# Six norm factors in the projection stage of a hybrid encoder layer: spread over the partitions by a round trip through DRAM where matmuls with an identity did it

## Chip, cores, metric

One Trainium2 chip, one core. The metric is the device time of one execution in microseconds, taken over several runs; a lower time is better. A profile was taken of one execution.

## What is computed

One encoder layer over 2048 tokens of width 1024, and a last norm. Cut to what matters here:

```python
h = rmsnorm(x, g_attn)                 # a factor per token: rsqrt(mean(x*x) + 1e-6)
p = h @ w_in                           # 2816 columns
a_b, a_c, a_h = p[0:768]               # mixer A: y_a = a_b * conv3(a_c * a_h)
b_glu = p[768:1280]                    # mixer B:
g = b_glu[:256] * sigmoid(b_glu[256:])
g = causal_dwconv(g, w_conv_b) + b     #   31 taps in depth
y_b = silu(layernorm(g, ln_g, ln_b))   #   mean and a factor per token over 256 channels
q, k, v = p[1280:2816]                 # mixer C: stick-breaking attention, 8 heads of 64
x = x + concat(y_a, y_b, y_c) @ w_out
h2 = rmsnorm(x, g_ffn)
x = x + relu(h2 @ w_ff1)**2 @ w_ff2
return rmsnorm(x, g_final)
```

## The kernel before

Everything is kept transposed: 128 channels on the partitions, 512 tokens along the free dimension, four such blocks of tokens (0 to 3). Each product in full precision is made of three TensorE matmuls in float32r (high by high, low by high, high by low; `mm3`, lines 103, 105 and 107). So each 128x512 output of the projection takes 24 matmuls, and a "group" below is one of these.

**The projection stage** runs in two halves (`p_half(0)`, blocks 0 and 1; `p_half(1)`, blocks 2 and 3). A half goes through eleven weight units: two for mixer B (G), three for mixer A, two each for K, Q and V. Outputs go into PSUM banks with the tag "d", of which there are three, so the TensorE can be at most three groups ahead of the VectorE, which takes each output out of PSUM (`p_evac`, `p_v`). Beside the projection, `weave` advances other generators in step with it: `mixer_b` (the 31 taps on the VectorE, which adds into one PSUM bank with the tag "c", and the layer norm), `x_norms` (sums of squares of x for blocks 2 and 3, in the first half), in the second half the attention of the first token block and `pre_split` (later weights are split into high and low and written to DRAM). A table of numbers in the call of `weave` (cost, start, end) says how fast each is advanced. A scheduler then sets each engine's order of instructions by that program order, by priorities (`tc.high_priority`) and by a simulated timeline; on the chip each engine runs its row strictly in order.

**The attention pieces** need PSUM banks with the tag "z", of which there are two. For each head `a_pass1` asks for three score tiles (`ps_z`, lines 528 and 529) and `a_cross` for one more (`ps_t`, lines 637 to 656, a chain of small VectorE steps). A score tile of the next head has to wait until the VectorE has finished with the bank that it is given.

**The norm factors.** A norm's sum over channels is made by a matmul with ones (`colsum`, line 127), which leaves the sums of 512 tokens as a 128x4 tile: token on the partition. The VectorE scales it (`rs_v`, line 115) and the Pool engine raises it to -1/2 (`rs_y`, line 118). The factor is needed along the free dimension and on all partitions, since the tokens lie there. Before, `spread` does this: four matmuls per norm, each with a column of `rs_y` broadcast as one operand and a 128x128 identity as the other, all in plain float32, into a PSUM tile `ps_R` (line 134). In `norm_spread` the ScalarE copies `ps_R` to an SBUF tile `R` (line 273), which every later evacuation of that token block multiplies by. In `mixer_b` the VectorE multiplies both channel halves (`cb`, line 484) by `ps_R` in PSUM directly; `ps_R` there takes the only "c" bank, in which the next block's taps also add up.

Twelve norms are spread in this way in the program. The six that the change touches are those of `x_norms` (blocks 2 and 3) and of `mixer_b` (blocks 0 to 3). The first two of the projection (`norm_x`), and the four of the later blocks stay as they are.

**Queues.** Loads and stores issued by `self.dma` stand on the queue of the SyncE (SP), which issues in order: where one waits, all behind it wait. `load_r` and the stores of mixer B's output are issued by the Pool engine, in order among its vector instructions.

Of the kernel before, what the change touches and what calls it, by code (L numbers as in the profile page):

```python
# [7 lines left out]
F32 = mybir.dt.float32  # L8
# [7 lines left out]
P = 128  # L16
# [3 lines left out]
TB = 512  # L20
# [9 lines left out]
LN_EPS = 1e-5  # L30
# [38 lines left out]
class Trunk:  # L69
# [78 lines left out]
    def consts(self, ctx):  # L148
        nc, tc, a = self.nc, self.tc, self.a
        c = self.c = ctx.enter_context(tc.tile_pool(name="consts", bufs=1))  # L150
        self.tiny = ctx.enter_context(tc.tile_pool(name="tiny", bufs=2))
        self.dr = ctx.enter_context(tc.tile_pool(name="dr", bufs=1, space=DRAM))
        self.gvec = {}
        t = c.tile([P, DC], F32, name="g_attn")
        nc.scalar.dma_start(t, a["g_attn"].rearrange("(d p) -> p d", p=P))
        self.gvec["g_attn"] = t

        self.ident = c.tile([P, P], F32, name="ident")
        make_identity(nc, self.ident)
        self.ones2 = c.tile([P, 2], F32, name="ones2")  # L160
        nc.vector.memset(self.ones2, 1.0)
        self.mhalf = c.tile([P, 4], F32, name="mhalf")
        nc.vector.memset(self.mhalf, -0.5)
        self.KQ = self.dr.tile([H // 2, 2, P, 3, 2, S // 2], F32, name="KQ")
        self.VS = self.dr.tile([H, S, 2 * HD], F32, name="VS")
        self.Y = self.dr.tile([D, S], F32, name="Y")

        self.WS = self.dr.tile([len(UNITS), 2, P, DC, 256], F32, name="WS")


        self.split_w = {n: self.dr.tile([k, 2, P, 2, DC // 2, P], F32, name="s_" + n) for n, k in (("w_out", DC), ("w1", FC))}
        self.split_w["w2"] = self.dr.tile([FC // G, DC // 2, P, 2, G, 2, P], F32, name="s_w2")
# [71 lines left out]
    def x_norms(self):  # L244

        for g in (2, 3):
            ss = self.mx.tile([P, TB], F32, name="ss", tag="ss", bufs=2)
            for d in range(DC):
                t = self.rp.tile([P, TB], F32, name="xraw", tag=self.rt, bufs=self.rb)
                self.dma(t, self.a["xT"][d * P : (d + 1) * P, g * TB : (g + 1) * TB])  # L250
                self.x_square(ss, t, d, self.nc.gpsimd)
                yield 1
            self.ss[g] = ss
            self.norm_sum(g)
            for _ in range(3):
                yield 1
            self.norm_spread(g)
            yield 1

    def norm_x(self, g):  # L260
        with self.tc.high_priority(offset=HP):
# [185 lines left out]
    def mixer_b(self, hf):  # L447
        nc = self.nc
        for tb in (2 * hf, 2 * hf + 1):
            acc = []  # L450
            for c in range(2):
                while (c, tb) not in self.g:
                    yield None
                g = self.g[c, tb]
                t = self.psum("ps_c", "c")
                nc.vector.tensor_scalar(t, g[:, 0:TB], self.wb[:, c, 0:1], self.vb["b_conv_b"][:, c : c + 1], op0=ALU.mult, op1=ALU.add)
                for k in range(1, 31):
                    nc.vector.scalar_tensor_tensor(t, g[:, k : k + TB], self.wb[:, c, k : k + 1], t, op0=ALU.mult, op1=ALU.add)  # L458
                    if k % 3 == 0:
                        yield 1.8  # L460
                acc.append(self.mx.tile([P, TB], F32, name=f"cb{c}", tag="cb", bufs=2))
                nc.scalar.activation(acc[c], t, AF.Copy)
            for _ in range(3):
                yield 1.8
            mean = self.psum("ps_mean", "c")
            for c in range(2):
                nc.tensor.matmul(mean, self.avg, acc[c], start=c == 0, stop=c == 1)
            sqs = []
            for c in range(2):
                nc.vector.tensor_tensor(acc[c], acc[c], mean, op=ALU.subtract)  # L470
                sq = self.mx.tile([P, TB], F32, name="sq", tag="sq", bufs=2)
                nc.scalar.activation(sq, acc[c], AF.Square)
                sqs.append(sq)
            yield 1.8
            nc.gpsimd.tensor_tensor(sqs[0], sqs[0], sqs[1], op=ALU.add)
            for _ in range(2):
                yield 1.8
            yv = self.rsqrt(self.colsum(sqs[:1], "c"), 1.0 / 256.0, LN_EPS)
            for _ in range(4):
                yield 1.8  # L480
            R = self.spread(yv, "c")
            for c in range(2):
                gg, bb = self.vb["ln_b_g"][:, c : c + 1], self.vb["ln_b_b"][:, c : c + 1]
                nc.vector.tensor_tensor(acc[c], acc[c], R, op=ALU.mult)
                s = self.mx.tile([P, TB], F32, name="sq", tag="sq", bufs=2)
                nc.scalar.activation(s, acc[c], AF.Sigmoid, bias=bb, scale=gg)
                nc.scalar.activation(acc[c], acc[c], AF.Identity, bias=bb, scale=gg)
                nc.gpsimd.tensor_tensor(s, acc[c], s, op=ALU.mult)

                nc.gpsimd.dma_start(self.Y[256 + c * P : 256 + (c + 1) * P, tb * TB : (tb + 1) * TB], s)  # L490
                yield 1.8
# [568 lines left out]
    def build(self):  # L1060
        tc = self.tc
        with ExitStack() as ctx:
            self.consts(ctx)
            self.attention_consts(ctx)
            self.raw = ctx.enter_context(tc.tile_pool(name="raw", bufs=1))
            self.xb = 5
            self.presplit = [("w_out", c, q) for c in range(DC) for q in range(2)] + [("w1", c, q) for c in range(PRE) for q in range(2)]
            self.g, self.u, self.w, self.R, self.rv, self.sig, self.ca, self.ss, self.yraw = ({} for _ in range(9))
            with ExitStack() as c1:
                self.psum_pool(c1, d=3, c=1, z=2, q=1, o=1)  # L1070
                self.p_pools(c1)
                self.w_eng = "dve"
                self.sb = 2
                self.xl = [[None] * DC for _ in range(2)]
                self.xh = [[None] * DC for _ in range(2)]
                with tc.tile_pool(name="raw0", bufs=1) as self.rp:
                    self.rb, self.rt = 21, "raw"
                    self.p_start()
                self.rp = self.raw
                self.rb, self.rt = self.xb, "xt"  # L1080
                self.at = c1.enter_context(tc.tile_pool(name="at1", bufs=1))
                self.ab = dict(Kl=1, A0=6, om=2, Alo=2, Ahi=2, Vl=1, late=1, yc=2)
                weave(self.p_half(0), [(Side(self.mixer_b(0)), 115, 20, 225, True), (Side(self.x_norms()), 24, 60, 180, True)])
                self.heads = {}
                a0 = Side(self.attention([(h, 0) for h in range(H)]))
                weave(self.p_half(1), [(Side(self.mixer_b(1)), 116, 0, 200, True), (a0, 28, 0, 210, True), (Side(self.pre_split(self.presplit[:24])), 24, 0, 200, True), (Side(self.pre_split(self.presplit[24:])), len(self.presplit) - 24, 190, 230, True)])
            with ExitStack() as c2:
                self.psum_pool(c2, d=3, z=3, q=1, o=1)
                self.at = c2.enter_context(tc.tile_pool(name="at2", bufs=1, reuse_waits="tile"))
                self.st = c2.enter_context(tc.tile_pool(name="st2", bufs=1, reuse_waits="tile"))  # L1090
                self.ha = c2.enter_context(tc.tile_pool(name="ha", bufs=1, reuse_waits="tile"))
                self.hp = c2.enter_context(tc.tile_pool(name="hp", bufs=1, reuse_waits="tile"))
                self.ob = 2
                self.kmax = 1536
                self.ab = dict(Kl=1, A0=15, om=2, Alo=3, Ahi=3, Vl=2, late=2, yc=1)
                at = Side(self.attention([(h, i) for i in (1, 2, 3) for h in range(H)]))
                self.heads = {}

                def attend(i):
                    while self.heads.get(i, 0) < H:  # L1100
                        at.advance(at.done + 1)

                self.attend = attend
                self.end = iter(())
                for tb in range(4):
                    weave(self.block(tb, self.end), [(at, (74, 95, 107)[tb], 45, 365 if tb < 2 else 320, False)] if tb < 3 else [])
# [48 lines left out]
```

## Time and profile before

| | us |
|---|---|
| median of three runs | 2396.46 (2393.45 to 2396.71) |
| the profiled execution | 2389.55 |
| its span, first to last instruction | 2387.8 |
| its mean granted TensorE clock | 0.998 |

In the profile, a line of a timeline or of the chain of waits gives the start in us from the span's start, the time in us, the engine, the line of the program, and the operation with output and inputs; "xN" merges N neighbours. In a timeline square brackets give the idle time of that engine just before, and who ended it. A float32 matmul appears as two records, so one `spread` of four matmuls is "x8". Matmuls are pipelined: the recorded time of one runs on while the next has started, so what a matmul costs the TensorE is the distance between starts, not its recorded time. "PEld" is the loading of weights, "SPq" the issue of transfers by the SyncE.

### The profile page before, as it was taken

What the parts mean: (1) busy time and instruction counts of PE and PEld (TensorE: products, weight loads), DVE (VectorE), ACT (ScalarE), POOL (GpSimd) and SP (SyncE); (2) the same over time, 40 slices, a digit from 0 to 9 for tenths busy, and PEclk for the clock granted to TensorE, in tenths of its full rate; (3) what the DMA queues carried; (4) which work ended last, traced back from release to release, by engine and by line L of the source; (5) the groups of instructions that cost most, each with busy time, mean ns of one, the idle gap of its engine ahead of it and who ended that gap; (6) DMA issues with size and microseconds to landing.
All of it is one profiled execution on the core that took longest, in us unless ns stands there. A gap on an engine that the chain in (4) does not pass through costs nothing.

```text
span 2387.8 us, 32873 instructions
## 1 busy us (share of the span) xinstructions
PE 2369.9 (99%) x11316; PEld 2004.1 (84%) x11316; DVE 1500.4 (63%) x2492; ACT 1066.7 (45%) x2002; POOL 1151.7 (48%) x1231
## 2 busy tenths in 40 slices
PE   8999999999999999999999999999999999999998
PEld 7888988898888888888888888888888888888887
DVE  7966698943878777678766668586666525321114
ACT  5232433333566666545555555366555522311221
POOL 1342388731667666427666765278788710000000
PEclk9999999999999999999999999999999999999999
DMA  7569999888778777696677776856676557555545
GB/s 259 205 227 348 294 323 298 285 273 275 191 216 239 204 223 208 210 293 169 210 218 242 232 240 208 277 159 186 192 205 198 168 175 235 175 172 194 198 167 194
DMA packets 238984, 536.49 MB, mean 225 GB/s; under 512 B 27105, under 2 KB 100833, under 8 KB 223457
## 3 DMA queue, kind: packets, MB, share of 16 engines
q1 hardware_dynamic: 180304, 462.01, 57.9%
q0 software_dynamic: 39424, 62.93, 12.0%
q10 hardware_dynamic: 19088, 9.44, 1.4%
q8 instruction: 89, 1.46, 0.2%
q14 instruction: 79, 0.64, 0.1%
HBM read 386.19 MB, written 139.72 MB: 220 GB/s over the span
## 4 chain that ended last, share of the span: by engine, by line
PE 91%; DMA 3%; POOL 2%; issue 2%; DVE 1%; ACT 0%; SPq 0%; POOLq 0%; DVEq 0%; ACTq 0%
PE ps_u L103 10%; PE ps_y L103 10%; PE ps_u L105 10%; PE ps_u L107 10%; PE ps_y L105 10%; PE ps_y L107 10%; PE ps_p L107 4%; PE ps_p L105 3%; PE ps_p L103 3%; PE ps_z L528 3%; PE ps_z L529 3%; PE ps_x L107 2%; PE ps_x L103 2%; PE ps_x L105 2%; PE ps_o L735 2%; PE ps_o L734 2%
## 5 line engine op out<-in xcount | busy, mean ns | idle before, releaser
L90 POOL TENSOR_TENSOR Alo<-A,Ahi 128x512 fp32r<-128x512 f32 x288 | 383.7, 1343 | 90.5 <-ACT Ahi L88 54.3
L984 DVE TENSOR_TENSOR acc<-acc,ps_y 128x512 f32<-128x512 f32 (+1 forms) x264 | 176.0, 668 | 192.6 <-PE ps_y L107 190.2
L103 PE MATMUL ps_y<-fh,w 128*128 128x512 f32 (+1 forms) x1056 | 281.9, 385 | 0.0
L105 PE MATMUL ps_y<-fh,w 128*128 128x512 f32 (+1 forms) x1056 | 280.2, 384 | 0.0
L103 PE MATMUL ps_u<-hh,w 128*128 128x512 f32 x1024 | 278.9, 392 | 1.1 <-ACT hh L903 1.1
L107 PE MATMUL ps_y<-fl,w 128*128 128x512 f32 (+1 forms) x1056 | 279.7, 384 | 0.0
L105 PE MATMUL ps_u<-hh,w 128*128 128x512 f32 x1024 | 277.5, 390 | 0.0
L107 PE MATMUL ps_u<-hl,w 128*128 128x512 f32 x1024 | 277.1, 390 | 0.0
L623 POOL TENSOR_TENSOR A<-A,R 128x512 f32<-128x512 f32 x168 | 223.2, 1331 | 108.1 <-ACT A L621 90.8
L118 POOL TENSOR_TENSOR rs_y<-rs_v,mhalf 128x4 f32<-128x4 f32 (+1 forms) x13 | 13.2, 1017 | 480.5 <-DVE rs_v L117 437.7
L948 ACT ACTIVATE ps_u<-ps_u 128x512 f32<-128x512 f32 x128 | 74.6, 582 | 369.0 <-PE ps_u L107 362.1
L105 PEld LDWEIGHTS ps_y<-fh,w 128*128 128x128 f32 x1056 | 195.1, 188 | 39.6 <-DMA w<-wraw 0.4
L107 PEld LDWEIGHTS ps_y<-fl,w 128*128 128x128 f32 x1056 | 195.1, 188 | 38.8
L105 PEld LDWEIGHTS ps_u<-hh,w 128*128 128x128 f32 x1024 | 192.4, 188 | 40.5
L107 PEld LDWEIGHTS ps_u<-hl,w 128*128 128x128 f32 x1024 | 192.2, 188 | 39.9
L103 PEld LDWEIGHTS ps_y<-fh,w 128*128 128x128 f32 x1056 | 193.2, 188 | 36.5 <-DVE acc L984 0.2
L958 DVE TENSOR_TENSOR fl<-ps_u,fh 128x512 fp32r<-128x512 f32 x128 | 87.8, 686 | 210.6 <-ACT fh L957 210.1
L88 ACT ACTIVATE Ahi<-A 128x512 fp32r<-128x512 f32 x288 | 176.3, 625 | 92.7 <-PE ps_o L734 44.2
L103 PEld LDWEIGHTS ps_u<-hh,w 128*128 128x128 f32 x1024 | 187.5, 188 | 35.9 <-ACT hh L903 1.5
L625 DVE TENSOR_TENSOR R<-ps_z,R 128x512 f32<-128x512 f32 x168 | 115.7, 689 | 134.3 <-ACT ps_z L622 112.5
L458 DVE SCALAR_TENSOR_TENSOR ps_c<-g,wb,ps_c 128x512 f32<-128x512 f32 x240 | 180.1, 750 | 4.9
L90 DVE TENSOR_TENSOR w<-wraw,w 128x512 fp32r<-128x512 f32 x176 | 170.5, 993 | 19.4 <-ACT w L88 17.9
(179 smaller groups left out, 4749.0 us busy)
## 6 DMA issues: line engine op xcount, KB each, us to landing
w<-s_w SPq DMA_DIRECT2D x208, 512.0 KB, 4.0
wraw<-in_w SPq DMA_DIRECT2D x224, 256.0 KB, 4.7
w<-s_w SPq DMA_DIRECT2D x52, 1024.0 KB, 4.8
w<-s_w_out SPq DMA_DIRECT2D x64, 512.0 KB, 4.8
s_w<-w SPq DMA_DIRECT2D x48, 512.0 KB, 5.2
s_w<-w SPq DMA_DIRECT2D x24, 1024.0 KB, 5.9
Qd<-KQ SPq DMA_DIRECT2D x64, 256.0 KB, 6.1
xraw<-in_xT SPq DMA_DIRECT2D x48, 256.0 KB, 4.6
```

The lines of the kernel that those rows point to most:

```text
L88: nc.scalar.activation(hi, x, AF.Copy)
L90: e.tensor_tensor(lo, x, f(hi), op=ALU.subtract)
L103: self.nc.tensor.matmul(ps, wh, xh, start=start and k == 0, stop=False)
L105: self.nc.tensor.matmul(ps, wl, xh, start=False, stop=False)
L107: self.nc.tensor.matmul(ps, wh, xl, start=False, stop=stop and k == n - 1)
L458: nc.vector.scalar_tensor_tensor(t, g[:, k : k + TB], self.wb[:, c, k : k + 1], t, op0=ALU.mult, op1=ALU.add)
L528: nc.tensor.matmul(z[:, oc], keys, g["qh"][:, qc], start=k == 0, stop=False)
L623: nc.gpsimd.tensor_tensor(t, t, R, op=ALU.mult)
L625: nc.vector.tensor_tensor(Rn, z, R, op=ALU.mult)
L948: nc.scalar.activation(ps, ps, AF.Relu)
L958: nc.vector.tensor_tensor(lo, ps, f(hi), op=ALU.subtract)
L984: nc.vector.tensor_tensor(acc[d][:, cols], acc[d][:, cols], ps, op=ALU.add)
```

## The change

A small DRAM tile `NF[k]` (4 by 128) is made for each of the six norms. `put_factors` writes the 128x4 factors to it by a transfer issued by the Pool engine, turned so that the 512 tokens stand in a row; `all_factors` reads this row back by a transfer on the SyncE queue, with the row repeated for all 128 partitions, into an SBUF tile. For `x_norms` that tile is `R` itself, so the copy by the ScalarE goes too. For `mixer_b` it is a new tile `Rc` in the pool's buffers "sq" (two of them, shared with the squares and the sigmoids). The reading transfer has to wait until the writing one has landed. In `mixer_b` the steps between the factor and its use go from four to eight, and the numbers in `weave` follow.

```diff
+        self.NF = [self.dr.tile([4, P], F32, name=f"NF{k}") for k in range(6)]
...
             self.norm_sum(g)
+            self.put_factors(g + 2, self.rv[g])
             for _ in range(3):
                 yield 1
-            self.norm_spread(g)
+            self.R[g] = self.mx.tile([P, TB], F32, name="R", tag="Rs", bufs=4)
+            self.all_factors(self.R[g], g + 2)
             yield 1
+
+    def put_factors(self, k, y):
+        self.nc.gpsimd.dma_start(self.NF[k].rearrange("b p -> p b"), y)
+
+    def all_factors(self, t, k):
+        self.dma(t, self.NF[k].rearrange("b p -> (b p)").unsqueeze(0).to_broadcast([P, TB]))
...
-            yv = self.rsqrt(self.colsum(sqs[:1], "c"), 1.0 / 256.0, LN_EPS)
-            for _ in range(4):
+            self.put_factors(tb, self.rsqrt(self.colsum(sqs[:1], "c"), 1.0 / 256.0, LN_EPS))
+            for _ in range(5):
                 yield 1.8
-            R = self.spread(yv, "c")
+            R = self.mx.tile([P, TB], F32, name="Rc", tag="sq", bufs=2)
+            self.all_factors(R, tb)
+            for _ in range(3):
+                yield 1.8
...
-                weave(self.p_half(0), [(Side(self.mixer_b(0)), 115, 20, 225, True), (Side(self.x_norms()), 24, 60, 180, True)])
+                weave(self.p_half(0), [(Side(self.mixer_b(0)), 123, 20, 225, True), (Side(self.x_norms()), 24, 60, 180, True)])
...
-                weave(self.p_half(1), [(Side(self.mixer_b(1)), 116, 0, 200, True), ...
+                weave(self.p_half(1), [(Side(self.mixer_b(1)), 124, 0, 204, True), ...
```

From the end of the second half on, every engine's order is the same in both programs. Inside the two halves the orders differ, and three places show how. In the rows, names end in numbers that the build gives, and the lines of the changed program lie ten or thirteen higher.

The first place is the TensorE in the first half, where the factors of `mixer_b` for block 0 and of `x_norms` for block 2 are spread between two groups of unit 5 (K). Before:

```order
L107 MATMUL ps_p_1226<-xl1_6_461,wh5_955 128x512
L107 MATMUL ps_p_1226<-xl1_7_475,wh5_955 128x512
L134 MATMUL ps_R_1259<-ident_65,rs_y_1127 128x128 x4
L134 MATMUL ps_R_1277<-ident_65,rs_y_1136 128x128 x4
L103 MATMUL ps_p_1283<-xh1_0_377,wh5_955 128x512
```

The two rows of line 134 are gone in the changed program, and the group behind them follows the one ahead of them at once. In their stead the Pool engine's row now has, just behind the two powers of line 118:

```order
L118 TENSOR_TENSOR rs_y_1101<-rs_v_1102,mhalf_72 128x4
L118 TENSOR_TENSOR rs_y_1143<-rs_v_1144,mhalf_72 128x4
L244 TENSOR_TENSOR ss_1310<-ss_1310,xraw_1378 128x512
L83 DMA Kd_2554<-KQ_74 64x2x256
L265 DMA NF0_77<-rs_y_1101 128x4x1
L83 DMA Kd_2554<-KQ_74 64x2x256
L265 DMA NF4_81<-rs_y_1143 128x4x1
```

Both writes stand among loads of keys (`Kd`); the two reads stand next to one another on the SyncE's queue, between a store of K's high part and one of its low part.

The second place is the VectorE at that same norm. After the change it reads:

```order
L388 TENSOR_TENSOR kq_1261<-ps_p_1236,R_501 128x512
L468 SCALAR_TENSOR_TENSOR ps_c_1373<-g0_1_512,wb_338,ps_c_1373 128x512
L497 TENSOR_TENSOR cb0_712<-cb0_712,Rc_1234 128x512
L497 TENSOR_TENSOR cb1_956<-cb1_956,Rc_1234 128x512
L468 SCALAR_TENSOR_TENSOR ps_c_1373<-g0_1_512,wb_338,ps_c_1373 128x512 x3
L388 TENSOR_TENSOR kq_1296<-ps_p_1271,R_501 128x512
```

The multiplications by the factor now stand between taps of the next block (line 468, adding into `ps_c`): these no longer wait for the bank, and one evacuation (`kq`) stands four rows behind the multiplications. Before, the taps of the next block began only behind them.

The third place is the VectorE in the second half, at block 2's norm, where heads of the attention run beside it. Before, this is the row from the scaled sum (`rs_v`) to the first tap of block 3, with rows left out in the middle:

```order
L115 TENSOR_SCALAR rs_v_3545<-ps_ss_3539 128x4
L371 TENSOR_TENSOR ya_3659<-ps_p_3634,ca_3614 128x512
L709 TENSOR_TENSOR yc_3623<-yc_3623,ps_o_3450 64x512
L637 STREAM_TRANSPOSE ps_t_3560<-R_3372 128x512
...
L656 TENSOR_TENSOR T_3561<-T_3561,ps_t_3560 128x512
...
L484 TENSOR_TENSOR cb0_2921<-cb0_2921,ps_R_3662 128x512
L484 TENSOR_TENSOR cb1_3309<-cb1_3309,ps_R_3662 128x512
...
L456 TENSOR_SCALAR ps_c_3804<-g0_3_2799,wb_332,b_conv_b_334 128x512
```

And after the change:

```order
L669 TENSOR_TENSOR T_3556<-T_3556,ps_t_3555 128x512
...
L115 TENSOR_SCALAR rs_v_3487<-ps_ss_3481 128x4
L381 TENSOR_TENSOR ya_3654<-ps_p_3629,ca_3609 128x512
L466 TENSOR_SCALAR ps_c_3857<-g0_3_2793,wb_338,b_conv_b_340 128x512
...
L652 SCALAR_TENSOR_TENSOR T_3875<-d1_90,ps_t_3874 128x512
L497 TENSOR_TENSOR cb0_2915<-cb0_2915,Rc_3657 128x512
L497 TENSOR_TENSOR cb1_3303<-cb1_3303,Rc_3657 128x512
```

The head whose chain (line 656, now 669) stood behind `rs_v` now stands ahead of it, block 3's taps begin right behind `rs_v`, and the multiplications by the factor stand 28 rows behind it, in the midst of the next head's chain (line 652 is the scan of `a_cross`). On the TensorE the score tiles follow: the three score tiles of the fourth to sixth heads stand 5 to 29 matmuls of the projection earlier in its row than before.

More of the change, by code (lines that the diff above doesn't have):

```diff
@@ L1082, in build @@
                 self.ab = dict(Kl=1, A0=6, om=2, Alo=2, Ahi=2, Vl=1, late=1, yc=2)
-                weave(self.p_half(0), [(Side(self.mixer_b(0)), 115, 20, 225, True), (Side(self.x_norms()), 24, 60, 180, True)])
+                weave(self.p_half(0), [(Side(self.mixer_b(0)), 123, 20, 225, True), (Side(self.x_norms()), 24, 60, 180, True)])
                 self.heads = {}
                 a0 = Side(self.attention([(h, 0) for h in range(H)]))
-                weave(self.p_half(1), [(Side(self.mixer_b(1)), 116, 0, 200, True), (a0, 28, 0, 210, True), (Side(self.pre_split(self.presplit[:24])), 24, 0, 200, True), (Side(self.pre_split(self.presplit[24:])), len(self.presplit) - 24, 190, 230, True)])
+                weave(self.p_half(1), [(Side(self.mixer_b(1)), 124, 0, 204, True), (a0, 28, 0, 210, True), (Side(self.pre_split(self.presplit[:24])), 24, 0, 200, True), (Side(self.pre_split(self.presplit[24:])), len(self.presplit) - 24, 190, 230, True)])
             with ExitStack() as c2:
```

## The prediction

> **What bounds the kernel now.** First the page's table of engines, then the shares of the chain of waits by engine:
>
> ```profile
> PE 2369.9 (99%) x11316; PEld 2004.1 (84%) x11316; DVE 1500.4 (63%) x2492; ACT 1066.7 (45%) x2002; POOL 1151.7 (48%) x1231
> ...
> PE 91%; DMA 3%; POOL 2%; issue 2%; DVE 1%; ACT 0%; SPq 0%; POOLq 0%; DVEq 0%; ACTq 0%
> ```
>
> The TensorE is the bound, with 2369.9 of 2387.8 us. The change lies in the projection, so those stretches come next (busy time of each engine, clock, DMA share):
>
> ```profile
> 300.00:360.00 60.00, 60.00 (x285) 50.20 (x284) 56.05 (x92) 23.41 (x50) 54.00 (x58) 1.00 0.93 317
> 360.00:380.00 20.00, 19.86 (x97) 15.66 (x96) 13.81 (x23) 8.65 (x18) 18.65 (x21) 1.00 1.06 326
> 380.00:400.00 20.00, 19.25 (x97) 16.00 (x96) 19.29 (x32) 9.32 (x18) 16.57 (x19) 1.00 0.96 342
> 400.00:460.00 60.00, 60.00 (x286) 50.18 (x285) 57.49 (x101) 19.60 (x37) 43.80 (x54) 1.00 0.80 254
> ```
>
> The TensorE is full in all of them; the VectorE (third number) is nearly so: 56.05 of 60, 19.29 of 20, 57.49 of 60, with one loose stretch, 13.81 of 20. The granted clock is 1.00 throughout. Then the TensorE's waits from 100 to 560 us; there is one:
>
> ```profile
> PE ps_z L528 <- DVE T L656: 0.7, 1, 0.7
> ```
>
> So a TensorE instruction taken out here is worth its own time, as long as the VectorE does not become the one waited for.
>
> **What is removed.** Six spreads of four float32 matmuls are 24 matmuls, recorded as 48. The group's recorded time, from the groups of 100 to 560 us:
>
> ```profile
> L134 PE MATMUL ps_R<-ident,rs_y 128*128 128x128 f32 x48 | 6.2, 275 | 0.0
> ```
>
> The 6.2 us are not the saving: records of 275 ns overlap. What the TensorE gets back is the distance from the first start of a spread to the start behind it. Its timeline, one pair for each place (the first holds two spreads):
>
> ```profile
> 140.57 1.95 PE L134 MATMUL ps_R<-ident,rs_y 128*128 128x128 f32 x16
> 142.27 0.94 PE L103 MATMUL ps_p<-xh,wh 128*128 128x512 f32 x3
> ...
> 203.19 1.05 PE L134 MATMUL ps_R<-ident,rs_y 128*128 128x128 f32 x8
> 203.99 2.10 PE L103 MATMUL ps_p<-xh,wh 128*128 128x512 f32 x8
> ...
> 252.12 1.05 PE L134 MATMUL ps_R<-ident,rs_y 128*128 128x128 f32 x8
> 252.93 0.36 PE L403 MATMUL ps_v<-wh,xh 128*128 128x256 f32 x1
> ...
> 385.01 1.05 PE L134 MATMUL ps_R<-ident,rs_y 128*128 128x128 f32 x8
> 385.82 1.17 PE L105 MATMUL ps_p<-xh,wl 128*128 128x512 f32 x4
> 386.83 1.55 PE L107 MATMUL ps_p<-xl,wh 128*128 128x512 f32 x6
> 389.12 0.40 PE L528 MATMUL ps_z<-Qd,Kd 128*128 128x256 f32 x1 [0.74 <-DVE T L656]
> ...
> 496.46 1.05 PE L134 MATMUL ps_R<-ident,rs_y 128*128 128x128 f32 x8
> 497.26 0.36 PE L726 MATMUL ps_o<-Ahi,Vd 128*128 128x256 f32 x1
> ```
>
> 1.70 + 0.80 + 0.81 + 0.81 + 0.80 = 4.92 us, some 0.10 us per record. The Trainium skill, "TensorE: Matmul & The Clock Gate", section "Wait — 56ns, not 53.3ns?", gives 55.6 ns from start to start for a warm matmul with 128 columns. By it 48 records would give an estimated 2.7 us, and a time 2.2 us higher than mine; the trace shows about 0.10 us for each, and the measurement decides.
>
> The spread at 385 is a case by itself. 3.3 us behind it the TensorE waits 0.74 us for a VectorE step. If that step comes no earlier, the 0.81 us saved turn into a longer wait. The chain of waits agrees: it runs through the spreads at 140, 252 and 496, but at 385 through the VectorE:
>
> ```profile
> 385.00 1.69 DVE ca L364
> 386.74 1.73 DVE ca L366
> ...
> 390.35 1.15 PE ps_p L103 x5
> ```
>
> So 4.11 us are sure if nothing new waits, and 0 to 0.81 more. I take the middle, 4.5 us, since the change also moves VectorE work at that place, in a direction that may help (below).
>
> The two copies of `ps_R` by the ScalarE go too, and the multiplications read SBUF and not PSUM:
>
> ```profile
> L273 ACT ACTIVATE R<-ps_R x2: 575/586/597, 143.1 to 204.3; 128x512 f32<-128x512 f32 x2
> L484 DVE TENSOR_TENSOR cb<-cb,ps_R x8: 661/680/689, 141.7 to 498.2; 128x512 f32<-128x512 f32 x8
> ```
>
> The copies (2 × 0.59 us) lie beside TensorE work, the ScalarE being busy 23 of 60 us in the rows above: nothing. For the multiplications I take the same 0.68 us. The upper bound is another VectorE multiplication or addition of that size from two SBUF tiles, 0.99 us in the page's groups:
>
> ```profile
> L90 DVE TENSOR_TENSOR w<-wraw,w 128x512 fp32r<-128x512 f32 x176 | 170.5, 993 | 19.4 <-ACT w L88 17.9
> ```
>
> That would be 8 × 0.31 = 2.5 us of VectorE time, 0.6 us at each norm, not on the TensorE's path while evacuations have room. The lower bound is no change.
>
> **What is added.** Twelve DMAs: six writes on the Pool's queue, six reads on the SyncE's. No 2 KB write of single 4-byte elements stands in the trace. The nearest rows are two loads in that form (256 and 1024 single elements), and for the repeated read a load of the same 256 KB into 128 partitions; the last columns are KB and us from issue to landing:
>
> ```profile
> ln_b_g<-in_ln_b_g SPq DMA_DIRECT2D x1, 1.0 KB, 2.1
> g_ffn<-in_g_ffn SPq DMA_DIRECT2D x1, 4.0 KB, 5.0
> xraw<-in_xT SPq DMA_DIRECT2D x48, 256.0 KB, 4.6
> ```
>
> For 512 elements I take 3 us (ends 2.1 and 5.0), for the read 3 us (ends 2.1 and 4.6); six reads of 256 KB beside some 300 GB/s are 5 us of traffic spread over 360 us, so nothing. A handoff thus takes 4 to 10 us where the spread took about 1. The Trainium skill, "DMA: Bandwidth & Descriptors", "Rules for kernel authors", says that a strided last dimension becomes one descriptor per element and that a DMA reading what an earlier one wrote must await its completion; that speaks against this change, and the 2.1 and 5.0 us rows agree that small pieces cost microseconds. It bears on the late-factor rival below.
>
> What waits meanwhile? For `x_norms` (140 and 203) the factor is first used in the second half: hidden. For `mixer_b` blocks 0, 1 and 3 the VectorE has room: at block 0, whose factor was multiplied at 141.7, it waited for the TensorE soon after,
>
> ```profile
> 148.10 0.69 DVE L378 TENSOR_TENSOR kq<-ps_p,R 128x512 f32<-128x512 f32 x1 [0.35 <-PE ps_p L107]
> ```
>
> so that it had no arrears there. A late factor would stop the VectorE, but the TensorE only after up to three banks are full, 3 groups × 24 matmuls × 0.21 us (60.00 us / 285) = 15 us at most. For block 2 the chain is: the power, the write eight Pool instructions behind it, the read on SyncE's queue behind the store of `ya`, the multiplications. In the trace before:
>
> ```profile
> 383.45 1.03 POOL L118 TENSOR_TENSOR rs_y<-rs_v,mhalf 128x4 f32<-128x4 f32 x1
> ...
> 394.00 1.30 POOL L90 TENSOR_TENSOR wpl<-wraw,wph 128x512 fp32r<-128x512 f32 x1 [1.73 <-ACT wph L88]
> ...
> 395.74 0.43 SPq L79 DMA_DIRECT2D Y<-ya  x1
> ...
> 400.25 0.75 DVE L458 SCALAR_TENSOR_TENSOR ps_c<-g,wb,ps_c 128x512 f32<-128x512 f32 x1
> ...
> 409.80 0.68 DVE L378 TENSOR_TENSOR kq<-ps_p,R 128x512 f32<-128x512 f32 x1
> ```
>
> Eight Pool instructions of 0.4 to 1.3 us put the write near 392, its landing near 395, the read behind the store near 396 to 397, and its landing near 400. The multiplications now stand behind some 21 taps of 0.75 us and a dozen other rows, so near 404 to 408. The margin is 4 to 8 us with the middle prices, about 0 to 4 with the upper ones: I take it as hidden. The Pool spends on each write what it spent on another store,
>
> ```profile
> 149.68 0.61 POOL L490 DMA_DIRECT2D Y<-sq  x1
> ```
>
> and it is busy 43.80 of 60 us: hidden.
>
> **What is moved.** Taps of the next block no longer wait for the "c" bank, which fills the loose VectorE stretch at 360 to 380 (6.2 us idle) and makes the crowded one from 400 to 460 lighter. That can end the 0.74 us wait and the smaller gaps around it. On the other hand the score tiles of the fourth to sixth heads stand 5 to 29 matmuls earlier on the TensorE, 1 to 6 us at 0.21 us; unless the VectorE's chain of the head before comes as much earlier, the TensorE waits there. The order has this chain earlier too (line 669 ahead of `rs_v` and not behind). I put these two against each other at zero, with ends of 2 us gained and 4 us lost.
>
> **The sum.** 4.11 + 0.4 = 4.5 us saved. The profiled execution took 2389.55 us, 6.9 us under the median; 2385.05 on its basis, and on that of the median, 2396.46 − 4.5 = 2392.0 us. A difference of about 0.2% (4.8 us) is what a measurement of this kernel can tell from no change, so the forecast lies just inside it.
>
> **The rivals.**
>
> *More is gained.* The earlier taps relieve the VectorE, the wait at 389 and the small gaps around it go. For it speaks the idle 6.2 us at 360 to 380, that taps can fill; against it, that only 0.74 us of waiting are recorded at all. 4.92 + up to 2 = 5 to 7 us: 2389.5 to 2391.5.
>
> *Score tiles eat the gain.* The TensorE now reaches `ps_z` before the VectorE has given the bank back, as it did once at 389. The VectorE's 57.49 of 60 us says that it cannot run ahead by much; against it stands the moved chain. 0 to 4 us saved: 2392.5 to 2396.5.
>
> *The factor comes late at block 2* (the other side). If the Pool's eight instructions include one that waits (it idled 1.73 us for the ScalarE ahead of 394.00 before), or the 4-byte write costs 5 us or more beside weight traffic at DMA share 0.96, then the VectorE stands at the first multiplication, and behind it stand one more `kq` evacuation, taps and the scan's followers of a head. The TensorE loses time once the evacuation slack is used up: the group that starts at 450.89 needs the bank whose evacuation began at 449.23, so the slack there is
>
> ```profile
> 449.23 0.67 DVE L378 TENSOR_TENSOR kq<-ps_p,R 128x512 f32<-128x512 f32 x1
> ...
> 450.89 0.63 PE L103 MATMUL ps_p<-xh,wh 128*128 128x512 f32 x2
> ```
>
> 450.89 − 449.90 = 1.0 us. Each microsecond later than about 408 plus 1 then costs one; it decides from 4.5 us on, a landing later than about 413, and would be seen as slower from 9.3 us. With a landing at 415 to 425, 2 to 12 us lost net: 2398 to 2408.
>
> *The change does nothing for the time* (what the spreads free is waited away elsewhere): 2396.5. The chain's passing through the spreads at 140, 252 and 496 speaks against it.
>
> **How the numbers follow.** Forecast 0.40 (2391.5 to 2392.5); more gained 0.26; score tiles 0.19; late factor 0.10; nothing 0.05. Faster by over 0.2%: all of "more", and the third of the forecast's case that reaches 4.8 us with the runs' scatter: 0.26 + 0.14 = 0.40. Slower by over 0.2%: two thirds of "late", 0.07. The rest is same, 0.53. The range takes in the forecast, "more" and "score tiles" (0.85), and on both sides the runs' own scatter of 1.5 us (2393.45 to 2396.71) with a little of "late" at the upper end: 2386.5 to 2399.
>
> **What would show it.** Right: in the profile after, no line 134 between 100 and 560 us, the starts around the five places 0.8 us (1.7 at 140) closer, the TensorE's only waits there of 1 us or less, and no wait of line 497 on a DMA. More gained: no TensorE wait at all near 385. Score tiles: waits of `ps_z` on the VectorE's line 669 or 694 between 320 and 460. Late factor: a wait of line 497 on `Rc`, and behind it TensorE waits on `ps_p`. I would be wrong altogether if the stretch from 100 to 500 us came out longer than before, or more than 8 us shorter.

## The result, and the profile after

The changed kernel takes 2424.35 us (median; 2423.4 to 2427.6) where the kernel before took 2395.53 us in the same runs: a ratio of 1.0131, 95% interval 1.0118 to 1.0143. By the medians that is 29 us slower, by the ratio 31. Forecast were 2392.0 us in a range of 2386.5 to 2399, and the chance given to "slower" was 0.07.

The engine shares of the chain of waits, on the page after, to set beside those of before (91% on the TensorE):

```profile
PE 81%; DMA 8%; POOL 3%; DVE 3%; issue 3%; ACT 1%; SPq 0%; POOLq 0%; DVEq 0%; ACTq 0%
```

The TensorE's waits after from 60 to 560 us (in total, times, longest); before there was one, of 0.7 us:

```profile
PE ps_v L413 <- DVE vt L421: 19.0, 3, 8.8
PE ps_p L103 <- DVE kq L388: 4.1, 2, 2.7
PE ps_z L541 <- DVE R L591: 4.1, 4, 1.5
PE ps_o L739 <- DMA Vd<-VS: 2.3, 1, 2.3
```

Nineteen of some 31 us are three holes in the V units, where a group of matmuls is short. Below they are named by the time at which the waiting group starts in the kernel before: 223, 258 and 510 us (232, 275 and 543 after). The view by stretches shows the first two, and that the granted clock (third from the end) falls there. Behind the first hole the matmuls start 0.21 us apart from 232.3 to 235.9 us, and 0.12 us apart ahead of it and from 236 on:

```profile
220.00:260.00 40.00, 30.97 (x234) 29.66 (x233) 10.07 (x18) 9.30 (x18) 6.95 (x7) 0.87 0.99 319
260.00:300.00 40.00, 33.42 (x199) 30.19 (x197) 19.28 (x27) 20.32 (x37) 11.51 (x14) 0.91 0.78 217
```

The VectorE's and the SyncE's waits, and the time from issue to landing of the new transfers (last column, us), name what is late:

```profile
DVE cb L497 <- DMA Rc<-NF: 30.9, 3, 13.3
...
SPq L79 <- DMA NF<-rs_y: 37.6, 4, 14.8
...
Rc<-NF SPq DMA_DIRECT2D x4, 256.0 KB, 4.1
R<-NF SPq DMA_DIRECT2D x2, 256.0 KB, 7.0
NF<-rs_y POOLq DMA_DIRECT2D x6, 2.0 KB, 10.4
```

The writes of 2 KB take 10.4 us to land. The reads behind them stand still at the head of the SyncE's queue, and the stores of K behind the reads with them. Its timeline at the first handoff, nothing issued for 9.5 us:

```profile
137.05 1.33 SPq L79 DMA_DIRECT2D KQ<-khi  x1
147.91 0.33 SPq L79 DMA_DIRECT2D Rc<-NF  x1
148.75 0.33 SPq L79 DMA_DIRECT2D R<-NF  x1
149.17 0.38 SPq L79 DMA_DIRECT2D KQ<-klo  x1
```

And the VectorE and TensorE at block 1's norm (the hole of 258), where evacuations of V stand behind the multiplications:

```profile
270.98 1.29 DVE L497 TENSOR_TENSOR cb<-cb,Rc 128x512 f32<-128x512 f32 x2 [8.93 <-DMA Rc<-NF]
...
275.37 0.58 PE L413 MATMUL ps_v<-wh,xh 128*128 128x256 f32 x1 [6.00 <-DVE vt L421]
```

The largest hole, 8.82 us at 223, comes about in another way: no multiplication by a factor stands in its chain. The chain that leads up to its end runs through stores of K that land late (their median before is 4.8 us), and only then through the evacuations of V:

```profile
203.58 12.11 DMA KQ<-khi
...
215.76 8.02 DMA KQ<-khi
...
223.79 6.01 DMA KQ<-klo
...
231.27 0.48 ACT vt L420
...
231.78 0.49 DVE vt L421
```

The write of block 3's factor of `x_norms` is issued at 198.92, just ahead of it.

To see gain and loss apart, take the first matmul of each projection group in two timelines and subtract. For each group (named by its start before, us), the shift of its start against before; the last two columns belong to experiments that are described below:

| start before | after | 16-byte writes (rows16) | before + unread 4-byte writes (write4) |
|---|---|---|---|
| 135.1 | +0.33 | +0.36 | +0.28 |
| 142.3 | -1.37 | -1.34 | +0.28 |
| 197.7 | +0.17 | -1.46 | +0.28 |
| 204.0 | -0.63 | -2.27 | +0.28 |
| 223.6 | +8.69 | -2.39 | +1.70 |
| 249.2 | +10.73 | -2.05 | +5.64 |
| 252.9 | +9.93 | -2.85 | +5.64 |
| 261.6 | +18.89 | -2.34 | +9.48 |
| 299.7 | +20.76 | +0.48 | +9.57 |
| 359.8 | +23.17 | +2.20 | +10.10 |
| 463.0 | +26.70 | +3.11 | +16.01 |
| 536.6 | +34.13 | +3.04 | +20.04 |

The removed spreads give back 1.70, 0.80 and 0.80 us at 140, 203 and 252, as forecast; the loss comes between these places and behind them. Each column is one execution: write16 and w512x16, whose times below do not differ from that of the kernel before, stand at +1.92 and +4.86 at 536.6, so 2 to 5 us at the end of the table say little.

### The profile page after: what moved, and what is told of

It is laid out like the page before. It is cut to its first block, busy times and chain, and to the rows that moved or that the text cites. A ratio compares the mean times of both kernels' runs of the same rounds, so it can differ in the third digit from the quotient of the medians.

```text
span 2422.7 us, 32803 instructions
## 1 busy us (share of the span) xinstructions
PE 2374.2 (98%) x11268; PEld 2003.5 (83%) x11268; DVE 1512.2 (62%) x2492; ACT 1065.4 (44%) x2000; POOL 1153.6 (48%) x1237
## 3 DMA queue, kind: packets, MB, share of 16 engines
q8 instruction: 89, 1.46, 0.2%
## 4 chain that ended last, share of the span: by engine, by line
PE 81%; DMA 8%; POOL 3%; DVE 3%; issue 3%; ACT 1%; SPq 0%; POOLq 0%; DVEq 0%; ACTq 0%
PE ps_u L103 9%; PE ps_u L107 9%; PE ps_u L105 9%; PE ps_y L103 9%; PE ps_y L105 9%; PE ps_y L107 9%; PE ps_z L541 3%; PE ps_z L542 3%; PE ps_x L103 2%; PE ps_x L105 2%; PE ps_x L107 2%; PE ps_p L107 2%; PE ps_o L748 2%; PE ps_o L747 2%; PE ps_p L103 2%
```

## The experiments

Ratios are against the kernel before, timed in the same runs; its median there was 2392 to 2394 us, so 0.1% is 2.4 us. Where it is said that the orders are the same, every engine's row of instructions is.

**1. The write's shape alone (rows16).** The factors are written as they lie in SBUF, 128 rows of 16 bytes.

```diff
-self.NF = [self.dr.tile([4, P], F32, ...
+self.NF = [self.dr.tile([P, 4], F32, ...
-    self.nc.gpsimd.dma_start(self.NF[k].rearrange("b p -> p b"), y)
+    self.nc.gpsimd.dma_start(self.NF[k], y)
-    self.dma(t, self.NF[k].rearrange("b p -> (b p)").unsqueeze(0).to_broadcast([P, TB]))
+    self.dma(t, self.NF[k].rearrange("p b -> (p b)").unsqueeze(0).to_broadcast([P, TB]))
```

> The changed kernel with one thing different: the write leaves the factors in DRAM as they lie in SBUF, 128 rows of 16 bytes and not 512 single elements of 4; the read is the same row of 2 KB for 128 partitions, so the factors come out in another order of tokens (the output is not the reference's). Every engine's order is the same as in the changed kernel. Theory A (the time is lost to the 10 to 12 us that the write takes to land): the write lands in 2 to 4 us, the three waits of line 497 (8.6, 8.9, 13.3 us) shrink by 7 us each or vanish, the PE's 9 us holes at 223, 258 and 510 us too, and the time is 2392 to 2400. Theory B (the moved order of instructions loses the time, the write is a bystander): 2420 to 2426. Both: in between, with what is left standing at 300 to 480 us.

Measured: 2395.31 us, ratio 1.0010 (1.0002 to 1.0019). So 1.2% of 1.31%, some 29 us, hang on the shape of a 2 KB write. In this run the landing, and the VectorE's waits for the factors, are

```profile
NF<-rs_y POOLq DMA_DIRECT2D x6, 2.0 KB, 6.0
...
DVE cb L497 <- DMA Rc<-NF: 9.7, 3, 5.5
```

and the holes of 223, 258 and 510 us are gone (table above). That is theory A's number, though the landing is longer than the 2 to 4 us expected and the VectorE still waits 9.7 us for the factors, against 30.9. What it does not tell is whether the late landing costs by those who wait for it, or in another way. And 2 to 3 us are lost against before where 4 to 5 should be gained.

**2. Nobody waits for a write (no_wait, no_wait16).** The reads take a row of x; the writes stay, unread. Then the same with 16-byte writes, in the orders of no_wait.

```diff
-    self.dma(t, self.NF[k].rearrange("b p -> (b p)").unsqueeze(0).to_broadcast([P, TB]))
+    self.dma(t, self.a["xT"][k, 0:TB].unsqueeze(0).to_broadcast([P, TB]))
```

> The changed kernel with the six reads taking a row of x in place of the factors written (the writes stay; the numbers multiplied are other ones): nothing waits for a write any more. The scheduler puts some reads earlier. Theory A (waits for the write): 2395.5 - 4.9 = 2390.6, 2388 to 2394. Theory B (the moved order): 2398 or more, with TensorE waits on ps_z between 300 and 480 us as in the changed kernel.

> The kernel no_wait (reads of a row of x, that wait for no write) with its unread writes as 128 rows of 16 bytes; every engine's order is that of no_wait, which took 15 us more than before. Theory C (in no_wait only the 4-byte writes in the DMA engines cost): 2392 - 4 = 2388 (2386 to 2392), the stores of K and V landing in 3 to 5 us again. If no_wait lost by its own order or by the six reads of 256 KB: 2402 to 2408.

Measured: no_wait 2407.54 us, ratio 1.0069 (1.0055 to 1.0083), a miss of theory A as it then stood: nothing waits for a write, and 15 us are lost. The number is theory B's, but no_wait16, with the same orders, takes 2391.70 us, ratio 0.9995 (0.9986 to 1.0003), at the upper edge of theory C. So 0.74%, some 18 us, go to the 4-byte shape of writes that nobody reads. The multiplications still wait for the reads in both, 10.1 and 7.1 us in all.

**3. Writes added to the kernel before (write4, write16, w512x16, write4_act).** The spreads stay; behind each power a write is added that nobody reads. The DRAM tiles have the shape to match (not shown).

```diff
+            self.put_factors(g + 2, self.rv[g])
...
             yv = self.rsqrt(self.colsum(sqs[:1], "c"), 1.0 / 256.0, LN_EPS)
+            self.put_factors(tb, yv)
...
+    def put_factors(self, k, y):
+        self.nc.gpsimd.dma_start(self.NF[k].rearrange("b p -> p b"), y)      # write4
+        self.nc.gpsimd.dma_start(self.NF[k], y)                              # write16
+        self.nc.gpsimd.dma_start(self.NF[k].rearrange("b p c -> p b c"), y.unsqueeze(1).to_broadcast([P, 4, 4]))  # w512x16
+        self.nc.scalar.dma_start(self.NF[k].rearrange("b p -> p b"), y)      # write4_act
```

> The kernel before, spreads and all, with only the six writes of 512 single 4-byte elements added behind the powers; nobody reads them and nobody waits for them. Theory C (each such write keeps the DMA engines busy for some 10 us, and whatever else is transferred then lands 5 to 7 us late, on every queue): 2392.8 + 8 to 17 = 2401 to 2410, with stores of K and V landing in 8 to 12 us behind the writes. Theory A (only who waits for the write loses): 2392.8, within 2 us.

> The same, with the six writes as 128 rows of 16 bytes; every engine's order is the same as with the 4-byte writes. Theory C with the number of elements as the cause (128 and not 512): 2392 to 2396. If any write of the Pool's queue does harm, whatever its shape: 2400 or more.

> The kernel before with six unread writes again, each now of 512 separate pieces of 16 bytes (each factor four times over, in the place order of the 4-byte writes). Theory C1 (the number of pieces costs): as the 512 pieces of 4 bytes, landing in 10 to 13 us, 2393.5 + 15 to 25 = 2408 to 2418. Theory C2 (the 4 bytes cost, a piece of 16 is cheap): landing in 4 to 6 us, 2391 to 2396.

> The kernel before with the six unread writes of 512 single elements issued by the ScalarE, on its queue, in place of the Pool's. Theory C (the pieces fill the DMA engines, whichever queue they come by): stores and loads behind them land 5 us late again, 2403 to 2418, and the ScalarE's waits for the power add a little. If it is the Pool's queue that is slow with single elements: landing in 3 to 5 us, 2393 to 2397.

| | pieces of one write | landing, us | time, us | ratio (95%) |
|---|---|---|---|---|
| write4 | 512 of 4 bytes, Pool's queue | 12.3 | 2413.20 | 1.0082 (1.0069 to 1.0094) |
| write16 | 128 of 16 bytes, Pool's queue | 5.0 | 2391.18 | 0.9993 (0.9984 to 1.0002) |
| w512x16 | 512 of 16 bytes, Pool's queue | 6.0 | 2391.86 | 0.9997 (0.9988 to 1.0006) |
| write4_act | 512 of 4 bytes, ScalarE's queue | 11.4 | 2418.43 | 1.0107 (1.0093 to 1.0121) |

Six unread writes, 12 KB together, cost 20 us, more than the range that theory C gave; through the ScalarE's queue 26 us, in orders of its own. It is not the number of pieces (512 of 16 bytes cost nothing measurable), not the Pool's queue, and not the order: write4 and write16 have the same. The number of pieces is that of the access pattern; the trace counts 32 packets for each write on the Pool's queue, whatever its shape. The transfers' view from 193 to 209 us shows what happens; each number is the rate in a fortieth (0.4 us) of that stretch. Before:

```profile
GB/s 271 233 210 215 277 248 282 369 384 387 374 338 351 366 451 463 417 451 410 389 353 376 369 376 379 384 387 376 433 430 428 471 420 369 389 338 287 394 353 353
DMA packets 3766, 5.82 MB, mean 364 GB/s; under 512 B 258, under 2 KB 3139, under 8 KB 3508
...
KQ<-klo SPq DMA_DIRECT2D x6, 256.0 KB, 5.0
```

With the 4-byte writes (write4), where one is issued at 194.5 us (the first row is the engines' busy share in tenths):

```profile
DMA  8999999999999999990579846987932695679999
GB/s 174 248 248 297 353 353 351 371 335 320 387 357 361 344 410 228 74 84 0 20 46 87 46 44 41 102 61 61 123 41 41 102 184 102 256 297 405 387 374 376
DMA packets 2471, 3.40 MB, mean 212 GB/s; under 512 B 185, under 2 KB 2221, under 8 KB 2341
...
q1 hardware_dynamic: 2437, 3.38, 103.7%
q0 software_dynamic: 32, 0.00, 0.4%
...
KQ<-klo SPq DMA_DIRECT2D x4, 256.0 KB, 9.8
WS<-wh SPq DMA_DIRECT2D x1, 1024.0 KB, 13.2
```

With the 16-byte writes (write16):

```profile
DMA packets 3541, 5.72 MB, mean 358 GB/s; under 512 B 281, under 2 KB 2771, under 8 KB 3283
```

For 6 to 7 us the rate falls from above 350 to about 70 GB/s, while the engines are marked busy for more than half of that time, nearly all of it by the SyncE's transfers (queue q1, 103.7% over the stretch): these are held, and stores of K that took 5.0 us take 9.8. Why 4-byte pieces do this is not shown, nor whether it is their size alone or how close they lie in DRAM (pieces of all 128 partitions side by side make 512 bytes here and 2 KB in w512x16). The fall begins some 5 us behind the write's issue.

**4. Only one kind of norm (x_only, x_only16, b_only).** One half of the change is put back to spreads with the numbers of before; x_only16 is x_only with 16-byte writes, in the same orders.

```diff
# x_only: mixer_b as before
-            self.put_factors(tb, self.rsqrt(...))
...
+            R = self.spread(yv, "c")
# b_only: x_norms as before
-            self.put_factors(g + 2, self.rv[g])
...
+            self.norm_spread(g)
```

> Only the two norms of x_norms (blocks 2 and 3 of x) go by DRAM; mixer_b is as before, its numbers too. The factors are not used for 100 us. Theory A2 (the read waits at the head of the SyncE's queue and holds up the stores of K behind it): the SyncE waits some 10 us near 138 and some 8 us near 205, the VectorE and the TensorE follow near 223 with 9 to 11 us, and the time is 2395.5 - 1.65 + 10 = 2404 (2401 to 2407). Theory A1 (only the VectorE's wait for Rc matters): no loss, 2395.5 - 1.65 = 2394.

> Only the four norms of mixer_b go by DRAM; x_norms is spread as before. Theory A1 (the VectorE's wait for Rc, with the evacuations of V behind it): holes of 7 to 9 us near 258 and 510 stay, the one near 223 goes or shrinks, and the time is 2395.5 - 3.3 + 20 to 27 = 2412 to 2419. Theory A2 alone (the SyncE's queue): the loss of blocks 1 and 3 goes, 2400 to 2405.

> The kernel x_only (only x_norms by DRAM) with its two writes as rows of 16 bytes and every engine's order as in x_only, which took 16 us more than before; the factors come out in another order of tokens, so the output is not the reference's. If all of the 16 us came from the two 4-byte writes (queue and DMA engines): 2392 - 1.65 = 2390.4 (2389 to 2393). If the order of x_only has a part, as its TensorE waits on ps_z of 7.2 us near 336 and 356 may say: 2395 to 2401.

Measured: x_only 1.0068 (1.0055 to 1.0081), 2408.88 us; b_only 1.0114 (1.0101 to 1.0128), 2418.44 us; x_only16 1.0036 (1.0024 to 1.0048), 2402.98 us. b_only is theory A1's number, and as A1 had it the hole at 223 is gone there while those at 258 and 510 stay. The shifts of the groups tell the holes apart. At 223 the shift grows by 9.1 us in the changed kernel, 3.9 in x_only, 3.2 in no_wait and 0.3 in b_only: this hole comes with the writes of `x_norms`, waited for or not. At 258 (from 255.9 to 261.6) it grows by 9.0 us in the changed kernel, 9.2 in b_only and 1.1 in no_wait: this one is the wait for the factor. The two halves do not add up to the whole (0.68 + 1.14 against 1.31), and x_only lost more than A2 said. x_only16, somewhat above the range that was given to a part of the order, tells why: 0.32%, 8 us, go to the shape of its two writes; the other 8.6 us stay with the cheap write. Its groups come on time until 330 us (+0.67), and are +11.61 late at 359.8. The VectorE's timeline there, then the Pool's, then the TensorE's:

```profile
332.26 4.83 DVE L374 TENSOR_SCALAR ca<-u,wa 128x512 f32<-128x512 f32 x1
337.02 1.87 DVE L691 TENSOR_TENSOR A<-A,ps_q 128x512 f32<-128x512 f32 x3
...
348.37 0.78 DVE L374 TENSOR_SCALAR ca<-u,wa 128x512 f32<-128x512 f32 x1
```

```profile
332.68 1.31 POOL L90 TENSOR_TENSOR wpl<-wraw,wph 128x512 fp32r<-128x512 f32 x1
333.93 0.41 POOL L551 TENSOR_SCALAR_AFFINE_SELECT om<-om 128x256 f32<-128x256 f32 x1
334.28 0.62 POOL L551 TENSOR_SCALAR_AFFINE_SELECT A<-A 128x512 f32<-128x512 f32 x1
334.87 1.26 POOL L90 TENSOR_TENSOR wpl<-wraw,wph 128x512 fp32r<-128x512 f32 x1
336.09 0.71 POOL L600 TENSOR_TENSOR A<-A,om 128x256 f32<-128x256 f32 x1
336.76 1.24 POOL L83 DMA_DIRECT2D Kd<-KQ  x2
```

```profile
338.41 0.39 PE L736 MATMUL ps_o<-Ahi,Vd 128*128 128x256 f32 x1 [4.39 <-ACT Ahi L88]
```

One multiplication of 512 columns, which at 348.37 takes 0.78 us, lasts 4.83 us. It ends at 337.09, just behind the Pool's train of vector instructions (336.80); the next head's `A` is late by it, and the TensorE waits 4.39 us. Further on another lasts 7.37 us:

```profile
378.91 7.37 DVE L374 TENSOR_SCALAR ca<-u,wa 128x512 f32<-128x512 f32 x1
```

Before, the longest such step is 2.01 us, and the 24 steps that make `ca` (lines 364 and 366) take 24.7 us in all; in x_only16 they take 36.2 us. A longer VectorE step where the VectorE is full moves everything behind it.

**5. What takes the gain back with 16-byte writes (half_perm).** rows16, with blocks 2 and 3 of mixer_b spread again.

```diff
+            if hf == 0:
                 self.put_factors(tb, yv)
...
+            else:
+                ...
+                R = self.spread(yv, "c")
```

> rows16 with blocks 2 and 3 of mixer_b spread again, with the numbers of before; all orders stay near those of the changed kernel, not of before (the factors of the others come out in another order of tokens, so the output is not the reference's). Theory B for the last 6 us of rows16 (the order in the second half, with score tiles early on the TensorE): the waits on ps_z from 280 to 420 us stay, 2393.5 - 3.3 + 4 to 6 = 2394 to 2396. If the handoff of blocks 2 and 3 was what took the gain back: 2389.5 to 2391.5.

Measured: 2394.72 us, ratio 1.0008 (0.9999 to 1.0017): theory B's number, though no factor of the second half's `mixer_b` goes by DRAM. The waits on `ps_z` stay (3.4 us from 60 to 560 us). One `ca` step lasts 6.58 us at 390.8, but the groups' shift does not grow by it (+5.38 at 381.8, +4.18 at 396.3). So the order of the second half, or the handoffs of the first, still cost the gain; that the handoff of blocks 2 and 3 adds nothing is not shown by it, since the intervals of both runs overlap.

**6. Versions that keep the tokens' order (half16, all16, late, half_view).** The 16-byte row has the tokens in another order, so its users read it with a stride. half16: x_norms and blocks 0 and 1, with a copy on the ScalarE for x_norms; late: the same with the copies written behind the first half; all16: all six; half_view: half16 without copies, the evacuations reading with a stride.

```diff
+ v = acc[c].rearrange("q (b p) -> q b p", b=4)
+ nc.vector.tensor_tensor(v, v, R.rearrange("q (p b) -> q b p", b=4), op=ALU.mult)
+ self.nc.scalar.activation(self.R[g].rearrange("q (b p) -> q b p", b=4), Rt.rearrange("q (p b) -> q b p", b=4), AF.Copy)
```

> A version with the right output: x_norms and mixer_b's blocks 0 and 1 by DRAM with 16-byte rows (the VectorE and one ScalarE copy read the row with a stride to put the tokens back), blocks 2 and 3 by spread with the numbers of before. The orders differ little from before. Saved are 1.70 + 0.80 + 0.81 = 3.3 us: 2389.5 (2388 to 2392). If the handoff still costs, as the 9.7 us of waits for Rc with 16-byte rows might: 2393 to 2398.

> All six norms by DRAM with 16-byte rows and the right output, with the waits and the weave numbers of before, so that the order in the second half is nearer to before than the changed kernel's. If the transfer is cheap now and the order was what cost rows16 its gain (theory B for the last 4 us): 2392.8 - 4.5 = 2388.3 (2387 to 2391). If blocks 2 and 3 lose by the handoff itself: 2392 to 2397, with waits of the multiplications for Rc and of the TensorE behind them.

> The version half16 with one change: the two ScalarE copies of x_norms' rows stand behind the first half and no longer in it, where one waited 4.83 us for its row and held up the split of V's weights. Every engine's order is otherwise near that of before. Saved: 1.70 + 0.80 + 0.81 = 3.3 us, 2390.2 (2388.5 to 2393). If the VectorE's waits for Rc at blocks 0 and 1 (4 to 5 us each) still reach the TensorE: 2394 to 2400.

> A version with the right output, as half16 but without a copy on the ScalarE: the evacuations of the second half read x_norms' rows with a stride. Saved by the spreads 3.3 us: 2388.8 (2387 to 2392) if strided reads hide on the VectorE. The scheduler makes another order of it than before, near that of rows16: 2393 to 2396 if theory B (order) holds, more if the strided evacuations (1.09 us against 0.69 us each) slow the VectorE at 300 to 460 us, where it is full.

Measured: half16 1.0034 (1.0021 to 1.0046), all16 1.0035 (1.0024 to 1.0047), late 1.0040 (1.0027 to 1.0053), half_view 1.0044 (1.0032 to 1.0056), 2401 to 2404 us each. All missed their gain of 3 to 5 us. In half16 the ScalarE stands 4.83 us before the copy, and the split of V's weights and the evacuations behind it, which shows at 223 us as +4.19. In late the copy was written elsewhere, but the scheduler put it in the same place, so that run did not test what it should. In half_view strided evacuations take 1.05 to 1.15 us where others take 0.68, and `ca` steps of 4.84 and 6.2 us come back. None of them beats the kernel before.

## Why the prediction was wrong

The sign that the prediction named for being wrong altogether came: the stretch from 100 to 500 us is longer, the group at 493.6 starting 26.19 us later than before, with waits of line 497 on a transfer. Two steps failed, the price of a write and the effect of a write on other transfers, which was no term of the sum.

- **The removed term was right.** Of the 4.11 us called sure, 1.70, 0.80 and 0.80 us appear in rows16 and after, and 1.24 us at 497, where 0.80 were put.
- **"For 512 elements I take 3 us (ends 2.1 and 5.0)" is the first step that failed.** The two nearest rows were loads into SBUF made of single elements. The change writes single elements to DRAM, and such a write lands in 10.4 us after, in 12.3 us in write4. A load was taken for a store; the direction was not weighed, though no run tests that the direction is what makes the difference. At blocks 0, 1 and 3, where the factor was taken to come early enough, it now came late. At block 2, for which the margin of "4 to 8 us" had been worked out, the margin held: the read was issued at 425.74, and the multiplications began at 434.56 without a wait, since the VectorE itself was late there (3.86 us of waiting for a store of `ya`, ahead of 430.91).
- **"six reads of 256 KB ... so nothing", and the same for the writes, is the second.** Transfers were priced by their bytes and their own landing. What a small transfer does to the others was no term at all. It is the largest: 18 us (no_wait against no_wait16), 20 us in write4. The hole at 223, the largest, is of this kind.
- **The late-factor rival named a mechanism that is part of the loss, and block 2, the one place where it did not happen.** Line 497 waited at blocks 0, 1 and 3 (30.9 us in three waits). "3 groups × 24 matmuls × 0.21 us", 15 us of cover, is an upper end for groups of 128x512 (at block 0 a wait of 8.62 us cost the TensorE 1.5 us, the shift going from -1.49 to +0.02 at 164.2); the norms of blocks 1 and 3 lie in the V units, where matmuls of 256 columns follow every 0.12 us, so the cover there is 3 × 24 × 0.12 = 8.6 us at most, and the waits were 8.93 and 13.33 us.
- **The SyncE's queue was looked at for the read's own time, and not for what stands behind it.** In the trace after it waits 37.6 us for the writes, with K's stores behind. By the ratios of after and no_wait (1.0131 against 1.0069), waiting costs another 0.62%, some 15 us; since the orders of these two differ, and no_wait still waits for its reads, that share is rough.
- **The moved order** was put at zero with ends of 2 us gained and 4 lost. rows16, with all orders of the changed kernel, ends 2.4 us slower and not 4.5 faster: some 7 us lost to order and cheap handoff together. The rival "score tiles eat the gain" holds in kind: `ps_z` waits for the VectorE, 3.7 us in rows16. A `ca` step of 5.3 us stands there at 387.6, but the next wait on `ps_z` comes at 419.9, so that it has a part in these waits is not shown. What exactly takes the 7 us stays open.
- The sentence cited from the Trainium skill's "DMA: Bandwidth & Descriptors" (single elements, one descriptor each) pointed the right way and gave no size. If the count of descriptors were the measure, 512 pieces of 16 bytes would be as bad; w512x16 shows no cost for them.

## What to carry to other kernels

Price a small transfer by its smallest piece, and look for a row of that very kind, in the same direction; where none is in the trace, a load is no upper bound for a store. Count what a slow transfer does to all others in flight, and what stands in the queue behind the one that waits for it. A VectorE stall is covered by as many groups as there are banks, so take the length of the groups at that place, not the common one; and where an engine is full, a gain of 4 us is no more than a new order can take.

## What the runs showed of the hardware that was not expected

- A write of 512 single 4-byte elements to DRAM lands in 10 to 12 us and holds other transfers for 6 to 7 us (rate from above 350 to about 70 GB/s); 512 pieces of 16 bytes land in 6.0 us, and cost nothing measurable.
- A VectorE step that works from SBUF to SBUF can last several times its length beside a train of Pool instructions: 4.83 us (to just behind five of them, 332.68 to 336.80 us) and 7.37 us (378.91 to 386.28, beside seven) for steps of 0.7 to 0.8 us. In the 17 traces 217 VectorE steps last over 1.5 us longer than the median of their line. Beside each of them the Pool is at work for at least 74% of its time, and none reads or writes PSUM. The kernel before has such steps too, further on (4.36 us at 984.97, line 90). The Trainium skill, "SBUF — State Buffer", section "SBUF: two separate sides", says that a pair of ports which the VectorE and the GpSimd share goes, by an exclusive lock and for a whole instruction, to whichever starts first: a GpSimd instruction, or a VectorE one that is in a two-port mode or, against a GpSimd one that reads SBUF, has two inputs there. The trace agrees in kind; that one step waits for five Pool instructions in a row, all of which start behind its own recorded start (332.26), is more than that sentence says. No run took the Pool's train away, so this cause is read from timelines and not tested.
- Behind a hole of 6 to 9 us in the TensorE's row its granted clock is lower for a while (0.87 and 0.91 in the two stretches of 40 us that hold the holes of 8.82 and 6.00 us), so the hole costs more than its length: behind the one of 8.82 us at 223 the groups' shift went from -0.38 (start before 220.7) to +10.39 us (227.8).
